# Layernorm of x + residual on one core: loads ahead of the opening barrier, no closing barriers, compute loops of 4 rows instead of 8

## The chip, the cores and the metric

The kernel runs on one core of one Trainium2 chip. The metric is the time of one execution in device microseconds (us). Each execution also has a *span*: the time from the first to the last instruction that the profiler recorded on that core. The timed figure is longer than the span of the same execution by 1.3 to 2.2 us; this document calls the difference *the time outside the span*, and it turns out to matter.

The engines are PE (matrix products), ACT, DVE and POOL (arithmetic on rows), and SP, which here only issues transfers; a *q* behind a name (SPq) marks instructions of the engine's own sequencer, PEld the loading of weights. A *DMA* is a transfer between memory and the chip's buffers. A *barrier* lets no engine go on before all have reached it; a *drain* is an instruction that stands in front of one. A *turn* is one pass of a loop, and a *junk buffer* takes an output that nobody reads, where only the accumulated sum is wanted.

## The reference, cut to what matters

```python
batch, seq, dim = 16, 1024, 512          # x, residual: float32; out: float32
z = x + residual
mean = np.mean(z, axis=-1, keepdims=True)
var  = np.var(z, axis=-1, keepdims=True)
return gamma * (z - mean) / np.sqrt(var + eps) + beta
```

There are 16,384 rows of 512 elements. With 128 partitions, each partition holds 128 rows; "a row" below means one such row on all partitions (256 KB). Two inputs are read and one output is written, 100.67 MB in all.

## The kernel before

The kernel is written by hand inside a critical section of a tile context: every engine has its own instruction stream, and semaphores tie them together. SP issues all large DMAs on one queue; POOL adds; ACT computes mean and sum of squares; DVE normalizes in place; SP stores. These are the parts that the change touches:

```python
TURN = 8                                  # rows per iteration of the ACT and DVE loops
JUNK = 4
...
ctx.enter_context(tc.tile_critical())
...
for c, (lo, n) in enumerate(loads_x):     # SP: loads of 8 rows (2 MB), stores of 16 rows (4 MB),
    ...                                   # at the end stores of 8, 4 and 4 rows
    nc.sync.dma_start(out=part(zbuf, Z_ROWS, lo, n), in_=dram(xf, lo, n)).then_inc(sx[c], 16)
    ...
with act.Fori(0, turns) as t:             # ACT, 8 rows a turn
    act.wait_ge(s_add, r0 + TURN)
    for k in range(2 * TURN):             # 8 means, then 8 sums of squares
        ...
        i.then_inc(s_act, 1).wait_op(s_act, due, "sem-ge")
    act.activation(out=std[...], in_=ssq[...], func=ACT.Sqrt, ...)...
with dve.Fori(0, turns) as t:             # DVE, 8 rows a turn
    for k in range(TURN):
        ...                               # each row waits for its own sum of squares
        dve.scalar_tensor_tensor(... nm ... gamma_p ...).wait_op(s_act, due, "sem-ge")
    dve.reciprocal(...)
    for k in range(TURN):
        dve.scalar_tensor_tensor(... rstd ... beta_p ...).then_inc(s_out, 1)
for o, (lo, n) in enumerate(stores):      # SP: wait for the last stores, clear all semaphores
    if lo >= stored:
        nc.sync.wait_ge(so[o], 16)
...
nc.sync.sem_clear(range(nums[0], nums[-1] + 1))
# leaving the critical section and the tile context adds the closing barriers
```

Of the kernel before, what the change touches and what calls it, by code (L numbers as in the profile page):

```python
# [6 lines left out]

FP32 = mybir.dt.float32
ACT = mybir.ActivationFunctionType
ALU = mybir.AluOpType  # L10


X_CHUNKS = [8] * 15 + [4, 4]
R_CHUNKS = [8] * 15 + [4, 4]
OUT_CHUNKS = [16] * 7 + [8, 4, 4]

Z_ROWS = 64
R_ROWS = 32
STORE_LAG = 40


TURN = 8


JUNK = 4


@with_exitstack
def kernel(
# [9 lines left out]
    nc = tc.nc  # L39
    P = nc.NUM_PARTITIONS  # L40
    xf = x.flatten_outer_dims()
    rf = residual.flatten_outer_dims()
    of = out.flatten_outer_dims()
    N, D = xf.shape
    inv_d = 1.0 / float(D)
    total = N // P
    turns = total // TURN

    def spans(sizes):
        assert sum(sizes) == total  # L50
        return [(sum(sizes[:c]), n) for c, n in enumerate(sizes)]

    blocks = spans(OUT_CHUNKS)

    def dram(t, lo, n):

        b0, bn = next(b for b in blocks if b[0] <= lo and lo + n <= b[0] + b[1])
        v = t[P * b0 : P * (b0 + bn), :].rearrange("(p j) d -> p j d", p=P)
        return v[:, lo - b0 : lo - b0 + n, :].rearrange("p a b -> p (a b)")

    ctx.enter_context(tc.tile_critical())  # L61

    zbuf = nc.alloc_sbuf_tensor("zbuf", [P, Z_ROWS * D], FP32)
    rbuf = nc.alloc_sbuf_tensor("rbuf", [P, R_ROWS * D], FP32)
    gb_row = nc.alloc_sbuf_tensor("gb_row", [1, 2 * D], FP32)
# [3 lines left out]
    nm = nc.alloc_sbuf_tensor("nm", [P, total], FP32)  # L69
    ssq = nc.alloc_sbuf_tensor("ssq", [P, total], FP32)  # L70
# [1 line left out]
    rstd = nc.alloc_sbuf_tensor("rstd", [P, total], FP32)  # L72
    gamma_p = nc.alloc_psum_tensor("gamma_p", [P, D], FP32)
    beta_p = nc.alloc_psum_tensor("beta_p", [P, D], FP32)
    junk = [nc.alloc_psum_tensor(f"junk{i}", [P, D], FP32) for i in range(JUNK)]

    sems = []

    def sem(name):
        s = nc.alloc_semaphore(name)  # L80
        sems.append(s)
        return s

    loads_x, loads_r, stores = spans(X_CHUNKS), spans(R_CHUNKS), spans(OUT_CHUNKS)
    sx = [sem(f"sx{c}") for c in range(len(loads_x))]
    sr = [sem(f"sr{c}") for c in range(len(loads_r))]
    so = [sem(f"so{c}") for c in range(len(stores))]
    s_gb = [sem(f"gb{k}") for k in range(2)]
    s_const = sem("const")
    s_pe = sem("pe")  # L90
    s_add = sem("add")
    s_act = sem("act")
    s_std = sem("std")
    s_dve = sem("dve")
    s_out = sem("out")

    def part(buf, size, lo, n):
        assert lo % size + n <= size
        return buf[:, (lo % size) * D : (lo % size + n) * D]


    nc.scalar.dma_start(out=gb_row[:, :D], in_=gamma[None, :]).then_inc(s_gb[0], 16)
    nc.scalar.dma_start(out=gb_row[:, D:], in_=beta[None, :]).then_inc(s_gb[1], 16)
    nc.vector.memset(ones[:, :], 1.0).then_inc(s_const, 1)  # L104
    nc.vector.memset(eps_t[:, :], float(eps)).then_inc(s_const, 1)  # L105
    nc.tensor.wait_ge(s_const, 1)
# [6 lines left out]

    todo_r, todo_o = list(enumerate(loads_r)), list(enumerate(stores))
    seen = {"add": 0, "out": 0}

    def wait_rows(s, key, rows):
        if rows > seen[key]:
            nc.sync.wait_ge(s, rows)
            seen[key] = rows  # L120

    stored = 0
    for c, (lo, n) in enumerate(loads_x):
        asked = lo + n
        while stored < asked - Z_ROWS:
            o = next(i for i, b in enumerate(stores) if b[0] == stored)
            assert all(o != t[0] for t in todo_o)
            nc.sync.wait_ge(so[o], 16)
            stored += stores[o][1]
        nc.sync.dma_start(  # L130
            out=part(zbuf, Z_ROWS, lo, n), in_=dram(xf, lo, n)
        ).then_inc(sx[c], 16)
        while todo_r and todo_r[0][1][0] + todo_r[0][1][1] <= asked:
            rc, (rlo, rn) = todo_r.pop(0)
            wait_rows(s_add, "add", rlo + rn - R_ROWS)
            nc.sync.dma_start(  # L136
                out=part(rbuf, R_ROWS, rlo, rn), in_=dram(rf, rlo, rn)
            ).then_inc(sr[rc], 16)
        while todo_o and (
            todo_o[0][1][0] + todo_o[0][1][1] <= asked - STORE_LAG or asked == total  # L140
        ):
            oc, (olo, on) = todo_o.pop(0)
            wait_rows(s_out, "out", olo + on)
            nc.sync.dma_start(  # L144
                out=dram(of, olo, on), in_=part(zbuf, Z_ROWS, olo, on)
            ).then_inc(so[oc], 16)


    have_x = have_r = 0
    lo = 0  # L150
    while lo < total:
        n = min(loads_x[have_x][1], loads_r[have_r][1])
        nc.gpsimd.wait_ge(sx[have_x], 16)
        nc.gpsimd.wait_ge(sr[have_r], 16)
        assert loads_x[have_x] == loads_r[have_r] == (lo, n)
        z = part(zbuf, Z_ROWS, lo, n)
        nc.gpsimd.tensor_tensor(  # L157
            out=z, in0=z, in1=part(rbuf, R_ROWS, lo, n), op=ALU.add
        ).then_inc(s_add, n)
        have_x, have_r, lo = have_x + 1, have_r + 1, lo + n  # L160

    def row_at(zoff, k):
        return zbuf[:, bass.ds(zoff + k * D, D)]


    act = nc.scalar
    act.preload_act_table_set("sqrt_and_others")  # L167
    act.wait_ge(s_const, 2)
    act.sem_inc(s_act, JUNK)
    with act.Fori(0, turns) as t:  # L170
        zoff = act.snap((t * (TURN * D)) % (Z_ROWS * D))
        r0 = act.snap(t * TURN)

        n0 = act.snap(t * (2 * TURN))
        act.wait_ge(s_add, r0 + TURN)
        for k in range(2 * TURN):
            row = k % TURN


            due = act.lower_val(n0 + (k + 1))  # L180
            if k < TURN:
                i = act.activation(  # L182
                    out=junk[k % JUNK][:, :],
                    in_=row_at(zoff, row),
                    func=ACT.Identity,
                    scale=-inv_d,
                    accum_out=nm[:, bass.ds(r0 + row, 1)],
                )
            else:
                i = act.activation(  # L190
                    out=junk[k % JUNK][:, :],
                    in_=row_at(zoff, row),
                    func=ACT.Square,
                    bias=nm[:, bass.ds(r0 + row, 1)],
                    accum_out=ssq[:, bass.ds(r0 + row, 1)],
                )
            i.then_inc(s_act, 1).wait_op(s_act, due, "sem-ge")
        due = act.lower_val(n0 + (JUNK + 2 * TURN))
        act.activation(  # L199
            out=std[:, bass.ds(r0, TURN)],  # L200
            in_=ssq[:, bass.ds(r0, TURN)],
            func=ACT.Sqrt,
            bias=eps_t[:, 0:1],
            scale=inv_d,
        ).then_inc(s_std, TURN).wait_op(s_act, due, "sem-ge")


    dve = nc.vector
    dve.wait_ge(s_pe, 2)
    with dve.Fori(0, turns) as t:  # L210
        zoff = dve.snap((t * (TURN * D)) % (Z_ROWS * D))
        r0 = dve.snap(t * TURN)
        n0 = dve.snap(t * (2 * TURN))
        for k in range(TURN):
            due = dve.lower_val(n0 + (JUNK + TURN + k + 1))
            dve.scalar_tensor_tensor(  # L216
                out=row_at(zoff, k),
                in0=row_at(zoff, k),
                scalar=nm[:, bass.ds(r0 + k, 1)],
                in1=gamma_p[:, :],  # L220
                op0=ALU.add,
                op1=ALU.mult,
            ).wait_op(s_act, due, "sem-ge")
        due = dve.lower_val(r0 + TURN)
        dve.reciprocal(  # L225
            out=rstd[:, bass.ds(r0, TURN)], in_=std[:, bass.ds(r0, TURN)]
        ).then_inc(s_dve, TURN).wait_op(s_std, due, "sem-ge")
        for k in range(TURN):
            i = dve.scalar_tensor_tensor(  # L229
                out=row_at(zoff, k),  # L230
                in0=row_at(zoff, k),
                scalar=rstd[:, bass.ds(r0 + k, 1)],
                in1=beta_p[:, :],
                op0=ALU.mult,
                op1=ALU.add,
            )
            i.then_inc(s_out, 1)
            if k == 0:
                i.wait_op(s_dve, due, "sem-ge")


    for o, (lo, n) in enumerate(stores):
        if lo >= stored:
            nc.sync.wait_ge(so[o], 16)
    nums = sorted(s.num for s in sems)
    assert nums == list(range(nums[0], nums[-1] + 1)), nums
    nc.sync.sem_clear(range(nums[0], nums[-1] + 1))


# [33 lines left out]
```

## Time and profile before

| | before |
|---|---|
| timed, median of 3 | 242.63 us (242.59 to 242.68) |
| profiled execution: timed / span | 242.21 / 240.03 us |
| DMA in the middle (24 to 180 us) | 430 GB/s |
| ACT, DVE, POOL busy | 74%, 74%, 59% |
| first load issued / its first packet | 0.94 / 1.96 us |
| last packet / last store's semaphore seen / end of span | 238.29 / 238.77 / 240.03 us |

The view by windows gives, for a stretch of time (us from the span's start), its length, the busy time of PE, PEld, DVE, ACT and POOL with the number of instructions, the clock, the mean busy share of the 16 DMA engines, and GB/s. Of the kernel before:

```profile
24.00:180.00 156.00, 0.00 (x0) 0.00 (x0) 137.24 (x209) 139.00 (x420) 105.70 (x13) 1.00 1.01 430
228.00:231.00 3.00, 0.00 (x0) 0.00 (x0) 3.00 (x5) 0.00 (x0) 0.00 (x0) 1.00 1.02 437
231.00:234.00 3.00, 0.00 (x0) 0.00 (x0) 0.11 (x1) 0.00 (x0) 0.00 (x0) 1.00 0.97 410
236.00:238.00 2.00, 0.00 (x0) 0.00 (x0) 0.00 (x0) 0.00 (x0) 0.00 (x0) 1.00 0.45 188
238.00:239.00 1.00, 0.00 (x0) 0.00 (x0) 0.00 (x0) 0.00 (x0) 0.00 (x0) 1.00 0.00 0
239.00:240.00 1.00, 0.00 (x0) 0.00 (x0) 0.00 (x0) 0.00 (x0) 0.00 (x0) 1.00 0.00 0
```

The DMA is saturated until about 236 us, even while the last rows are computed (228 to 231). The Trainium skill ("DMA: Bandwidth & Descriptors", Specifications) gives 435 GB/s as the ceiling of the fabric between the 16 DMA engines and the on-chip buffer; the 430 GB/s here agree. From 238 us on, nothing is moved and nothing is computed, yet the span goes on for two microseconds.

What fills these microseconds is in the sequencers' instructions. For one line of the source, this view gives engine, operation, count, shortest/median/longest duration in ns, and the start of the first and of the last one in us. Line 278 is the tile context, line 247 the clearing of semaphores:

```profile
L247 SPq EVENT_SEMAPHORE_RANGE_CLEAR  x1: 115/115/115, 238.8 to 238.8; - x1
...
L278 POOLq EVENT_SEMAPHORE  x4: 17/17/17, 239.4 to 239.9; - x4
...
L278 SPq DRAIN  x3: 7/7/7, 239.3 to 239.6; - x3
...
L278 SPq EVENT_SEMAPHORE  x2: 17/17/17, 239.5 to 240.0; - x2
```

After the last store's semaphore at 238.77, SP clears (238.83), and then two rounds of drains and barriers of the tile context follow, preceded by a handshake of the critical section. Each instruction takes 7 to 115 ns; from 238.77 to the end of the span it is 1.26 us.

The start, in the timeline (start us, duration us, engine, line, operation; lines of other engines cut):

```profile
0.94 0.39 SPq L130 DMA_DIRECT2D zbuf<-in_x_dram  x1
...
1.38 0.43 SPq L136 DMA_DIRECT2D rbuf<-in_residual_dram  x1
...
1.86 0.42 SPq L130 DMA_DIRECT2D zbuf<-in_x_dram  x1
```

Finally the compute loop. In the chain that ended last (start us, duration us, what), ACT's seven merged steps of sums of squares come once a turn:

```profile
30.77 2.32 ACT junk L190 x7
...
42.20 2.32 ACT junk L190 x7
...
53.59 2.31 ACT junk L190 x7
```

So a turn of 8 rows takes ACT 42.20 - 30.77 = 11.43 us. The DMA needs 6.29 MB / 430 GB/s = 14.6 us for the same rows, so compute has slack.

### The profile page before, as it was taken

The numbers are of one execution on the slowest core, as the hardware profiler recorded it, in microseconds if no ns is written. First come the engines' busy times: TensorE is split into PE (matmuls) and PEld (weight loads), VectorE is DVE, ScalarE is ACT, GpSimd is POOL, SyncE is SP. The second block draws the span as 40 slices with busy tenths as digits, with TensorE's granted clock in tenths as the row PEclk, the third lists the DMA queues.
The fourth block names the chain that finished last, engine by engine and source line by source line (L and its number), as shares of the span: only waits on it lengthen the run. The fifth ranks groups of instructions, "written<-read, shape, count | busy, mean of one in ns | idle before, by whom it ended". The sixth has DMA issues, their size and how long they took to land.

```text
span 240.0 us, 1853 instructions
## 1 busy us (share of the span) xinstructions
PE 4.1 (2%) x4; PEld 1.0 (0%) x4; DVE 178.7 (74%) x274; ACT 176.6 (74%) x529; POOL 142.2 (59%) x21
## 2 busy tenths in 40 slices
PE   3300000000000000000000000000000000000000
PEld 0000000000000000000000000000000000000000
DVE  0000399999999999999997399944999359995950
ACT  2002999999999999999972999449993599959500
POOL 0078989889899506894088920989109890860000
DMA  7999999999999999999999999999999999999994
GB/s 252 434 420 429 431 435 431 429 415 431 434 440 437 415 420 431 475 437 390 429 434 434 420 426 434 429 453 426 415 423 431 456 399 423 445 426 431 431 418 205
DMA packets 6341, 100.68 MB, mean 419 GB/s; under 512 B 706, under 2 KB 706, under 8 KB 708
## 3 DMA queue, kind: packets, MB, share of 16 engines
q1 hardware_dynamic: 6336, 100.67, 98.4%
q14 instruction: 1, 0.01, 0.0%
q10 hardware_dynamic: 4, 0.00, 0.0%
HBM read 67.11 MB, written 33.55 MB: 419 GB/s over the span
## 4 chain that ended last, share of the span: by engine, by line
DMA 56%; ACT 14%; issue 14%; POOL 6%; DVE 3%; SPq 2%; ACTq 2%; DVEq 0%; POOLq 0%
DMA out_dram<-zbuf 36%; DMA rbuf<-in_residual_dram 20%; ACT junk L190 9%; POOL zbuf L157 6%; ACT junk L182 5%; DVE zbuf L229 3%; SPq L130 1%; ACTq L180 1%; ACTq L182 1%; SPq L136 1%; ACT std L199 0%; SPq L144 0%; DVE rstd L225 0%; DVEq L229 0%; ACTq L170 0%
## 5 line engine op out<-in xcount | busy, mean ns | idle before, releaser
L157 POOL TENSOR_TENSOR zbuf<-zbuf,rbuf 128x4096 f32<-128x4096 f32 (+1 forms) x17 | 142.0, 8351 | 71.5 <-DMA rbuf<-in_residual_dram 71.5
L216 DVE SCALAR_TENSOR_TENSOR zbuf<-zbuf,nm,gamma_p 128x512 f32 x128 | 91.0, 747 | 50.8 <-ACT junk L190 50.8
L182 ACT ACTIVATE junk<-zbuf 128x512 f32 x128 | 74.4, 581 | 45.3 <-POOL zbuf L157 41.6
L229 DVE SCALAR_TENSOR_TENSOR zbuf<-zbuf,rstd,beta_p 128x512 f32 x128 | 85.7, 743 | 0.6
L190 ACT ACTIVATE junk<-zbuf,nm 128x512 f32 x128 | 86.1, 673 | 0.0
L190 ACT ACTIVATION_READ_ACCUMULATOR junk<-zbuf,nm x128 | 24.2, 189 | 0.0
L182 ACT ACTIVATION_READ_ACCUMULATOR junk<-zbuf x128 | 23.9, 187 | 0.0
L199 ACT ACTIVATE std<-ssq,eps_t x16 | 4.8, 301 | 1.6
L225 DVE RECIPROCAL rstd<-std x16 | 3.1, 196 | 0.0
L167 ACT ACT_TABLE_LOAD x1 | 1.3, 1283 | 1.7 <-SPq L61 1.7
L109 PE MATMUL beta_p<-gb_row,ones 1*128 1x512 f32 x2 | 2.1, 1136 | 2.4 <-DMA gb_row<-in_beta_dram 2.4
L109 PE MATMUL gamma_p<-gb_row,ones 1*128 1x512 f32 x2 | 2.0, 1122 | 2.3 <-DMA gb_row<-in_gamma_dram 2.3
L104 DVE MEMSET ones<- 1x128 f32 x1 | 0.2, 165 | 1.0 <-SPq L61 1.0
L109 PEld LDWEIGHTS beta_p<-gb_row,ones 1*128 1x128 f32 x2 | 0.5, 304 | 4.0 <-DMA gb_row<-in_beta_dram 4.0
L109 PEld LDWEIGHTS gamma_p<-gb_row,ones 1*128 1x128 f32 x2 | 0.5, 305 | 2.3 <-issue 2.3
L264 POOL MEMSET const-float32-0.0<- 128x1 f32 x1 | 0.1, 99 | 0.2 <-issue 0.2
L264 POOL MEMSET const-bfloat16-1.0<- 128x1 bf16 x1 | 0.1, 102 | 0.0
L264 POOL MEMSET const-uint8-127<- 128x1 uint8 x1 | 0.1, 102 | 0.0
L264 POOL MEMSET const-float32-1.0<- 128x1 f32 x1 | 0.1, 99 | 0.0
L105 DVE MEMSET eps_t<- 128x1 f32 x1 | 0.1, 59 | 0.0
## 6 DMA issues: line engine op xcount, KB each, us to landing
zbuf<-in_x_dram SPq DMA_DIRECT2D x15, 2048.0 KB, 32.8
rbuf<-in_residual_dram SPq DMA_DIRECT2D x15, 2048.0 KB, 30.4
out_dram<-zbuf SPq DMA_DIRECT2D x7, 4096.0 KB, 28.5
zbuf<-in_x_dram SPq DMA_DIRECT2D x2, 1024.0 KB, 32.6
rbuf<-in_residual_dram SPq DMA_DIRECT2D x2, 1024.0 KB, 34.6
out_dram<-zbuf SPq DMA_DIRECT2D x1, 2048.0 KB, 16.5
out_dram<-zbuf SPq DMA_DIRECT2D x2, 1024.0 KB, 7.7
gb_row<-in_gamma_dram ACTq DMA_DIRECT2D x1, 2.0 KB
```

The costliest lines, as they stand in the source:

```text
L109: nc.tensor.matmul(dest[:, :], ones[:, :], gb_row[:, k * D : (k + 1) * D], start=True, stop=True).then_inc(s_pe, 1)
L130: nc.sync.dma_start(out=part(zbuf, Z_ROWS, lo, n), in_=dram(xf, lo, n)).then_inc(sx[c], 16)
L136: nc.sync.dma_start(out=part(rbuf, R_ROWS, rlo, rn), in_=dram(rf, rlo, rn)).then_inc(sr[rc], 16)
L157: nc.gpsimd.tensor_tensor(out=z, in0=z, in1=part(rbuf, R_ROWS, lo, n), op=ALU.add).then_inc(s_add, n)
L167: act.preload_act_table_set("sqrt_and_others")
L180: due = act.lower_val(n0 + (k + 1))
L182: i = act.activation(out=junk[k % JUNK][:, :], in_=row_at(zoff, row), func=ACT.Identity, scale=-inv_d, accum_out=nm[:, bass.ds(r0 + row, 1)],)
L190: i = act.activation(out=junk[k % JUNK][:, :], in_=row_at(zoff, row), func=ACT.Square, bias=nm[:, bass.ds(r0 + row, 1)], accum_out=ssq[:, ...
L199: act.activation(out=std[:, bass.ds(r0, TURN)], in_=ssq[:, bass.ds(r0, TURN)], func=ACT.Sqrt, bias=eps_t[:, 0:1], scale=inv_d,).then_inc(s ...
L216: dve.scalar_tensor_tensor(out=row_at(zoff, k), in0=row_at(zoff, k), scalar=nm[:, bass.ds(r0 + k, 1)], in1=gamma_p[:, :], op0=ALU.add, op1 ...
L225: dve.reciprocal(out=rstd[:, bass.ds(r0, TURN)], in_=std[:, bass.ds(r0, TURN)]).then_inc(s_dve, TURN).wait_op(s_std, due, "sem-ge")
L229: i = dve.scalar_tensor_tensor(out=row_at(zoff, k), in0=row_at(zoff, k), scalar=rstd[:, bass.ds(r0 + k, 1)], in1=beta_p[:, :], op0=ALU.mul ...
```

## The change

Its intent: the first two loads shall be in flight before the opening barrier; nothing shall follow the last store but one small clear; the loops shall run 4 rows a turn with fewer register instructions. The tile context is closed and compiled empty at the kernel's start, so its barriers come first, and everything else is placed by hand behind it.

```diff
-TURN = 8
-JUNK = 4
+ADD = 8
+TURN = 4
+EARLY = 2
...
+    tc.close()
+    tc.compile()
...
-    ctx.enter_context(tc.tile_critical())
...
-    junk = [nc.alloc_psum_tensor(f"junk{i}", [P, D], FP32) for i in range(JUNK)]
+    junk_m = [...]        # one per row of a turn; two of the eight in SBUF
+    junk_s = [...]
...
+    def move(out, in_, s):
+        i = nc.sync.dma_start(out=out, in_=in_).then_inc(s, 16)
+        if len(first) < EARLY:
+            first.append(i.ins)
...
+    for o, (lo, n) in enumerate(stores[:-1]):
+        if lo >= stored:
+            nc.sync.wait_ge(so[o], 16)
+    nc.sync.sem_clear(range(nums[0], nums[-1]))
+    nc.sync.wait_ge(so[-1], 16)
+    nc.sync.sem_clear(range(nums[-1], nums[-1] + 1))
...
     # ACT: instead of a wait on every instruction
+        act.wait_ge(s_act, r0 * 2 + TURN)          # all means, then the squares
+        act.wait_ge(s_act, r0 * 2 + 2 * TURN)      # all squares, then the square root
...
     # DVE: instead of a wait on every row
+        dve.wait_ge(s_act, r0 * 2 + 2 * TURN)
...
+    blks = nc.main_func.blocks                     # the first two loads go ahead of the
+    names = {i.name for i in first}                # opening block's first Drain
+    ...
+    blks[0].instructions = opening[:at] + first + opening[at:]
```

More of the change, by code (lines that the diff above doesn't have):

```diff
@@ L6 @@
 from concourse._compat import with_exitstack
+from concourse.ordered_engine_set import OrderedEngineSet
 FP32 = mybir.dt.float32
@@ L74 @@
     beta_p = nc.alloc_psum_tensor("beta_p", [P, D], FP32)
-    junk = [nc.alloc_psum_tensor(f"junk{i}", [P, D], FP32) for i in range(JUNK)]
+    junk_m = [nc.alloc_psum_tensor(f"junk_m{i}", [P, D], FP32) for i in range(TURN)]
+    junk_s = [nc.alloc_psum_tensor(f"junk_s{i}", [P, D], FP32) for i in range(6 - TURN)]
+    junk_s += [
+        nc.alloc_sbuf_tensor(f"junk_s{i}", [P, D], FP32) for i in range(6 - TURN, TURN)
+    ]
     sems = []
@@ L82, in sem @@
         return s
-    loads_x, loads_r, stores = spans(X_CHUNKS), spans(R_CHUNKS), spans(OUT_CHUNKS)
+    loads_x, loads_r, stores = spans(X_CHUNKS), spans(R_CHUNKS), blocks
     sx = [sem(f"sx{c}") for c in range(len(loads_x))]
     sr = [sem(f"sr{c}") for c in range(len(loads_r))]
-    so = [sem(f"so{c}") for c in range(len(stores))]
     s_gb = [sem(f"gb{k}") for k in range(2)]
@@ L95 @@
     s_out = sem("out")
+    so = [sem(f"so{c}") for c in range(len(stores))]
+    nums = [s.num for s in sems]
+    assert nums == list(range(nums[0], nums[-1] + 1)), nums
     def part(buf, size, lo, n):
@@ L99, in part @@
         return buf[:, (lo % size) * D : (lo % size + n) * D]
-    nc.scalar.dma_start(out=gb_row[:, :D], in_=gamma[None, :]).then_inc(s_gb[0], 16)
-    nc.scalar.dma_start(out=gb_row[:, D:], in_=beta[None, :]).then_inc(s_gb[1], 16)
+    for k, src in enumerate((gamma, beta)):
+        nc.scalar.dma_start(out=gb_row[:, k * D : (k + 1) * D], in_=src[None, :]).then_inc(
+            s_gb[k], 16
+        )
     nc.vector.memset(ones[:, :], 1.0).then_inc(s_const, 1)
@@ L115 @@
     seen = {"add": 0, "out": 0}
+    first = []
     def wait_rows(s, key, rows):
@@ L129 @@
             stored += stores[o][1]
-        nc.sync.dma_start(
-            out=part(zbuf, Z_ROWS, lo, n), in_=dram(xf, lo, n)
-        ).then_inc(sx[c], 16)
+        move(part(zbuf, Z_ROWS, lo, n), dram(xf, lo, n), sx[c])
         while todo_r and todo_r[0][1][0] + todo_r[0][1][1] <= asked:
@@ L135 @@
             wait_rows(s_add, "add", rlo + rn - R_ROWS)
-            nc.sync.dma_start(
-                out=part(rbuf, R_ROWS, rlo, rn), in_=dram(rf, rlo, rn)
-            ).then_inc(sr[rc], 16)
+            move(part(rbuf, R_ROWS, rlo, rn), dram(rf, rlo, rn), sr[rc])
         while todo_o and (
@@ L143 @@
             wait_rows(s_out, "out", olo + on)
-            nc.sync.dma_start(
-                out=dram(of, olo, on), in_=part(zbuf, Z_ROWS, olo, on)
-            ).then_inc(so[oc], 16)
-    have_x = have_r = 0
-    lo = 0
-    while lo < total:
-        n = min(loads_x[have_x][1], loads_r[have_r][1])
-        nc.gpsimd.wait_ge(sx[have_x], 16)
-        nc.gpsimd.wait_ge(sr[have_r], 16)
-        assert loads_x[have_x] == loads_r[have_r] == (lo, n)
-        z = part(zbuf, Z_ROWS, lo, n)
-        nc.gpsimd.tensor_tensor(
-            out=z, in0=z, in1=part(rbuf, R_ROWS, lo, n), op=ALU.add
-        ).then_inc(s_add, n)
-        have_x, have_r, lo = have_x + 1, have_r + 1, lo + n
-    def row_at(zoff, k):
-        return zbuf[:, bass.ds(zoff + k * D, D)]
+            move(dram(of, olo, on), part(zbuf, Z_ROWS, olo, on), so[oc])
+    for o, (lo, n) in enumerate(stores[:-1]):
[4 more added lines that the diff above has]
+    nc.sync.sem_clear(range(nums[-1], nums[-1] + 1))
+    for c, (lo, n) in enumerate(loads_x):
+        nc.gpsimd.wait_ge(sx[c], 16)
+        for rc, (rlo, rn) in enumerate(loads_r):
+            if lo <= rlo < lo + n:
+                assert rlo + rn <= lo + n
+                nc.gpsimd.wait_ge(sr[rc], 16)
+                for a in range(rlo, rlo + rn, ADD):
+                    an = min(ADD, rlo + rn - a)
+                    z = part(zbuf, Z_ROWS, a, an)
+                    nc.gpsimd.tensor_tensor(
+                        out=z, in0=z, in1=part(rbuf, R_ROWS, a, an), op=ALU.add
+                    ).then_inc(s_add, an)
     act = nc.scalar
@@ L168 @@
     act.wait_ge(s_const, 2)
-    act.sem_inc(s_act, JUNK)
     with act.Fori(0, turns) as t:
@@ L172 @@
         r0 = act.snap(t * TURN)
-        n0 = act.snap(t * (2 * TURN))
         act.wait_ge(s_add, r0 + TURN)
-        for k in range(2 * TURN):
-            row = k % TURN
-            due = act.lower_val(n0 + (k + 1))
-            if k < TURN:
-                i = act.activation(
-                    out=junk[k % JUNK][:, :],
-                    in_=row_at(zoff, row),
-                    func=ACT.Identity,
-                    scale=-inv_d,
-                    accum_out=nm[:, bass.ds(r0 + row, 1)],
-                )
-            else:
-                i = act.activation(
-                    out=junk[k % JUNK][:, :],
-                    in_=row_at(zoff, row),
-                    func=ACT.Square,
-                    bias=nm[:, bass.ds(r0 + row, 1)],
-                    accum_out=ssq[:, bass.ds(r0 + row, 1)],
-                )
-            i.then_inc(s_act, 1).wait_op(s_act, due, "sem-ge")
-        due = act.lower_val(n0 + (JUNK + 2 * TURN))
+        for k in range(TURN):
+            act.activation(
+                out=junk_m[k][:, :],
+                in_=zbuf[:, bass.ds(zoff + k * D, D)],
+                func=ACT.Identity,
+                scale=-inv_d,
+                accum_out=nm[:, bass.ds(r0 + k, 1)],
+            ).then_inc(s_act, 1)
+        act.wait_ge(s_act, r0 * 2 + TURN)
+        for k in range(TURN):
+            act.activation(
+                out=junk_s[k][:, :],
+                in_=zbuf[:, bass.ds(zoff + k * D, D)],
+                func=ACT.Square,
+                bias=nm[:, bass.ds(r0 + k, 1)],
+                accum_out=ssq[:, bass.ds(r0 + k, 1)],
+            ).then_inc(s_act, 1)
+        act.wait_ge(s_act, r0 * 2 + 2 * TURN)
         act.activation(
@@ L204 @@
             scale=inv_d,
-        ).then_inc(s_std, TURN).wait_op(s_act, due, "sem-ge")
+        ).then_inc(s_std, TURN)
     dve = nc.vector
@@ L212 @@
         r0 = dve.snap(t * TURN)
-        n0 = dve.snap(t * (2 * TURN))
+        dve.wait_ge(s_act, r0 * 2 + 2 * TURN)
         for k in range(TURN):
-            due = dve.lower_val(n0 + (JUNK + TURN + k + 1))
+            row = zbuf[:, bass.ds(zoff + k * D, D)]
             dve.scalar_tensor_tensor(
-                out=row_at(zoff, k),
-                in0=row_at(zoff, k),
+                out=row,
+                in0=row,
                 scalar=nm[:, bass.ds(r0 + k, 1)],
@@ L222 @@
                 op1=ALU.mult,
-            ).wait_op(s_act, due, "sem-ge")
-        due = dve.lower_val(r0 + TURN)
+            )
+        dve.wait_ge(s_std, r0 + TURN)
         dve.reciprocal(
             out=rstd[:, bass.ds(r0, TURN)], in_=std[:, bass.ds(r0, TURN)]
-        ).then_inc(s_dve, TURN).wait_op(s_std, due, "sem-ge")
+        ).then_inc(s_dve, TURN)
+        dve.wait_ge(s_dve, r0 + TURN)
         for k in range(TURN):
-            i = dve.scalar_tensor_tensor(
-                out=row_at(zoff, k),
-                in0=row_at(zoff, k),
+            row = zbuf[:, bass.ds(zoff + k * D, D)]
+            dve.scalar_tensor_tensor(
+                out=row,
+                in0=row,
                 scalar=rstd[:, bass.ds(r0 + k, 1)],
@@ L235 @@
                 op1=ALU.add,
-            )
-            i.then_inc(s_out, 1)
-            if k == 0:
-                i.wait_op(s_dve, due, "sem-ge")
-    for o, (lo, n) in enumerate(stores):
-        if lo >= stored:
-            nc.sync.wait_ge(so[o], 16)
-    nums = sorted(s.num for s in sems)
-    assert nums == list(range(nums[0], nums[-1] + 1)), nums
-    nc.sync.sem_clear(range(nums[0], nums[-1] + 1))
+            ).then_inc(s_out, 1)
+    blks = nc.main_func.blocks
+    names = {i.name for i in first}
+    for b in blks[1:]:
+        kept = [i for i in b.instructions if i.name not in names]
+        if len(kept) < len(b.instructions):
+            b.instructions = kept
+    opening = list(blks[0].instructions)
+    at = next(n for n, i in enumerate(opening) if i.opcode == "Drain")
+    blks[0].instructions = opening[:at] + first + opening[at:]
 _INS = ['x', 'residual', 'gamma', 'beta', 'eps']
```

## The prediction

> **What bounds it now.** The DMA. The windows view gives 430 GB/s at a DMA share of about 1.00 from 24 to 180 us, and 423 to 441 in every window from 4 to 231. The Trainium skill ("DMA: Bandwidth & Descriptors", Specifications) gives 435 GB/s as the fabric ceiling of the 16 engines; this trace sits at it: 100.67 MB at 430 GB/s are 234 us of a 240.0 us span. ACT and DVE are busy 74% each, POOL 59%. One turn of 8 rows takes ACT 11.4 us where it runs without a gap (chain of waits, 23 to 80 us), but 8 rows are 6.29 MB, 14.6 us of DMA. Bytes issued against bytes landed: the queue never holds less than about 3.7 MB in the middle and 1.4 MB (3.3 us) at the end, so it never runs dry.
>
> What is not DMA is at the ends (timeline with the sequencers' instructions). The opening barrier and the jump take 0.0 to 0.82 us, the first load is issued at 0.94, its first packet is at 1.96. The last packet ends at 238.29, the last store's semaphore is seen at 238.77, and clearing semaphores (0.12 us) and closing barriers run until 240.0. The timed runs are 2.6 us longer than the span (242.63 against 240.0), which I carry over.
>
> **What the change does.**
> - First two loads ahead of the opening barrier: first issue from 0.94 to about 0.0, first packet from 1.96 to about 1.0. Two issues (0.39 + 0.43 us) delay the barrier for the rest, and the third load comes at perhaps 1.5 to 2.5 us; the 4.2 MB ahead of it last 9.8 us, so that is hidden. Critical: about -0.9 us.
> - No closing barriers: 238.77 to 240.03 is 1.26 us; one small clear remains, about 0.2. Critical: about -1.0 us. Engines done early might also shorten what follows the span; I count 0.2.
> - Turns of 4 rows: the ACT turn's fixed part is 11.39 - 8 x (0.61 + 0.71) = 0.85 us. Twice as many turns and a whole wait between means and squares give an estimated 12.7 us per 8 rows; DVE, which now starts after all squares, an estimated 12.5. Both stay under 14.6, so nothing reaches the DMA. At the end rows come out in finer pieces and the last stores are issued earlier, but the queue is not empty there in either kernel: worth 0.
> - Junk buffers in SBUF, semaphore order: off the path.
>
> **Prediction.** 242.63 - 0.9 - 1.0 - 0.2 is 240.5 us (0.991 of before). 8 in 10: 239.2 to 241.7. Faster by over 2% (below 237.8): 0.03; within 2%: 0.95; slower by over 2%: 0.02.
>
> **What would show it right.** First DMA issue at 0.0, first packet near 1.0 us; DMA still 428 to 432 GB/s in the middle; last packet near 237.4; the span ending 0.6 to 0.8 us after the last packet instead of 1.74, near 238.0. An ACT turn of 6.2 to 6.6 us. The large waits of the DMA queue stay waits for landed stores.
>
> **What would make it wrong.** The drain in the opening barrier might wait for the loads issued before it (about 10 us later): third load and compute start late, the queue runs dry, some us slower. The last engine's straggling packets (16 streams until 236.7, one until 238.3) may fall otherwise, +-0.7 us. A turn of 4 might cost ACT or DVE over 14.6 us per 8 rows. Or the time outside the span may change with the barriers.

## The result, and the profile after

Ratios here are the mean time of one kernel's runs over the mean of the other's runs of the same rounds, so they are not quite the ratio of the medians quoted.

| | before | after |
|---|---|---|
| timed, median of 4 | 242.61 us | 239.62 us (239.49 to 239.69) |
| ratio | | 0.9879, 95% interval 0.9862 to 0.9896 |
| profiled: timed / span | 242.21 / 240.03 | 239.69 / 238.37 |
| timed less span, same execution | 2.18 | 1.32 |
| first issue / first packet | 0.94 / 1.96 | 0.00 / 1.00 |
| last packet / end of span | 238.29 / 240.03 | 237.87 / 238.37 |

The windows of the kernel after:

```profile
24.00:180.00 156.00, 0.00 (x0) 0.00 (x0) 135.66 (x222) 144.72 (x426) 105.40 (x13) 1.00 1.01 430
...
228.00:231.00 3.00, 0.00 (x0) 0.00 (x0) 2.75 (x5) 0.00 (x0) 0.00 (x0) 1.00 0.97 415
231.00:234.00 3.00, 0.00 (x0) 0.00 (x0) 0.00 (x0) 0.00 (x0) 0.00 (x0) 1.00 0.99 418
234.00:236.00 2.00, 0.00 (x0) 0.00 (x0) 0.00 (x0) 0.00 (x0) 0.00 (x0) 1.00 0.98 414
236.00:238.00 2.00, 0.00 (x0) 0.00 (x0) 0.00 (x0) 0.00 (x0) 0.00 (x0) 1.00 0.06 25
238.00:238.40 0.40, 0.00 (x0) 0.00 (x0) 0.00 (x0) 0.00 (x0) 0.00 (x0) 1.00 0.00 0
```

The middle is unchanged at 430 GB/s. The share of 0.06 in the window 236 to 238 is about what a single DMA engine gives (one sixteenth is 0.0625); it works on alone after the others have finished.

The sequencers' instructions: line 169 is the last clear, line 55 the closing of the empty tile context, whose barriers now stand at the start:

```profile
L169 SPq EVENT_SEMAPHORE_RANGE_CLEAR  x1: 25/25/25, 238.3 to 238.3; - x1
...
L55 POOLq EVENT_SEMAPHORE  x4: 17/17/17, 1.4 to 1.8; - x4
...
L55 SPq DRAIN  x3: 7/7/7, 1.3 to 1.6; - x3
```

The start in the timeline:

```profile
0.00 0.38 SPq L138 DMA_DIRECT2D zbuf<-in_x_dram  x1
0.43 0.42 SPq L138 DMA_DIRECT2D rbuf<-in_residual_dram  x1
1.91 0.33 SPq L138 DMA_DIRECT2D zbuf<-in_x_dram  x1
```

ACT's merged steps of sums of squares in the chain that ended last; some groups between them are left out:

```profile
24.80 2.31 ACT junk_s L203 x7
...
31.02 2.31 ACT junk_s L203 x7
...
37.23 2.31 ACT junk_s L203 x7
```

The first two loads are issued at 0.00 and 0.43; the third waits until 1.91 for three barriers, but at its issue 4.2 MB are still outstanding, so the queue is not empty. SP's drain behind the two issues (0.91 us) took 125 ns, against 7 ns in before; it did not wait for the loads, which landed from 7.5 us on. A turn of 4 rows takes ACT 6.2 us (31.02 - 24.80), or 12.4 per 8 rows: more than the 11.4 of before, still below 14.6.

The profiles add up as follows. First packet: -0.96 us. From the last packet to the end of the span: 1.74 to 0.51, -1.24 us. From the first packet to the last: 236.33 to 236.87, +0.54 us. Together -1.66 us of span. Outside the span: -0.86 us. The sum is -2.52 us for these two executions. The profile of before was taken in one of its fastest executions (242.21, against medians of 242.38 to 242.88 in the later rounds), which makes the +0.54 look larger than it is on the average. It lies in the lag of one straggling DMA engine (last experiment): 1.52 us in this execution of after and 0.83 in this one of before.

### The profile page after: what moved, and what is told of

It reads as the page before. It is cut to its first block, busy times and chain, and to the rows that moved or that the text cites. A ratio compares the mean times of both kernels' runs of the same rounds, so it can differ in the third digit from the quotient of the medians.

```text
span 238.4 us, 1803 instructions
## 1 busy us (share of the span) xinstructions
PE 3.7 (2%) x4; PEld 1.2 (0%) x4; DVE 177.2 (74%) x290; ACT 186.5 (78%) x545; POOL 142.2 (60%) x21
## 4 chain that ended last, share of the span: by engine, by line
ACT 38%; DMA 33%; issue 10%; POOL 7%; ACTq 5%; DVE 3%; SPq 1%; DVEq 0%; POOLq 0%
DMA rbuf<-in_residual_dram 21%; ACT junk_s L203 20%; ACT junk_m L194 18%; DMA out_dram<-zbuf 12%; POOL zbuf L181 7%; ACTq L194 2%; DVE zbuf L228 2%; DVE zbuf L243 1%; ACTq L203 1%; SPq L138 1%; ACTq L189 1%; ACT std L211 0%; ACTq L201 0%; ACTq L210 0%; DVEq L228 0%
## 5 line engine op out<-in xcount | busy, mean ns | idle before, releaser
L228 DVE SCALAR_TENSOR_TENSOR zbuf<-zbuf,nm,gamma_p 128x512 f32 x128 | 87.1, 743 | 50.4 <-ACT junk_s L203 50.4
L194 ACT ACTIVATE junk_m<-zbuf 128x512 f32 x128 | 74.9, 585 | 28.5 <-POOL zbuf L181 23.3
L203 ACT ACTIVATE junk_s<-zbuf,nm 128x512 f32 x128 | 88.8, 694 | 3.9
L243 DVE SCALAR_TENSOR_TENSOR zbuf<-zbuf,rstd,beta_p 128x512 f32 x128 | 87.1, 744 | 1.1
L203 ACT ACTIVATION_READ_ACCUMULATOR junk_s<-zbuf,nm x128 | 23.9, 187 | 0.0
L194 ACT ACTIVATION_READ_ACCUMULATOR junk_m<-zbuf x128 | 23.9, 187 | 0.0
L211 ACT ACTIVATE std<-ssq,eps_t x32 | 9.5, 297 | 3.7
L237 DVE RECIPROCAL rstd<-std x32 | 5.4, 170 | 0.0
```

The lines of the kernel that those rows point to most:

```text
L194: act.activation(out=junk_m[k][:, :], in_=zbuf[:, bass.ds(zoff + k * D, D)], func=ACT.Identity, scale=-inv_d, accum_out=nm[:, bass.ds(r0 + ...
L203: act.activation(out=junk_s[k][:, :], in_=zbuf[:, bass.ds(zoff + k * D, D)], func=ACT.Square, bias=nm[:, bass.ds(r0 + k, 1)], accum_out=ss ...
L211: act.activation(out=std[:, bass.ds(r0, TURN)], in_=ssq[:, bass.ds(r0, TURN)], func=ACT.Sqrt, bias=eps_t[:, 0:1], scale=inv_d,).then_inc(s ...
L228: dve.scalar_tensor_tensor(out=row, in0=row, scalar=nm[:, bass.ds(r0 + k, 1)], in1=gamma_p[:, :], op0=ALU.add, op1=ALU.mult,)
L237: dve.reciprocal(out=rstd[:, bass.ds(r0, TURN)], in_=std[:, bass.ds(r0, TURN)]).then_inc(s_dve, TURN)
L243: dve.scalar_tensor_tensor(out=row, in0=row, scalar=rstd[:, bass.ds(r0 + k, 1)], in1=beta_p[:, :], op0=ALU.mult, op1=ALU.add,).then_inc(s_ ...
```

## The experiments

Twelve runs were made (eleven new kernels, and the kernel after once more), in three batches of five rounds on three chips. "Before" was timed in every batch: means 242.67, 242.82 and 242.38 us, spans 240.50, 240.65 and 240.20, outside the span 2.17, 2.16 and 2.18. The table gives each kernel's mean difference from before in its own rounds, split into span and outside; the last column is the mean time outside.

| run | timed, us | span | outside | time outside, us |
|---|---|---|---|---|
| after, run again | -2.71 | -1.85 | -0.86 | 1.32 |
| before, loads early | -0.72 | -0.74 | +0.02 | 2.19 |
| before, turns of 4 | -0.26 | +0.16 | -0.42 | 1.76 |
| same, ACT padded | -0.02 | +0.39 | -0.40 | 1.76 |
| same, DVE padded | +0.12 | +0.33 | -0.21 | 1.95 |
| before, ACT 4 rows, DVE 8 | +0.34 | +0.36 | -0.02 | 2.16 |
| after, no early loads | -1.24 | -0.37 | -0.87 | 1.30 |
| after, one barrier at the end | -1.93 | -1.56 | -0.37 | 1.80 |
| after, ACT and DVE padded | -2.70 | -1.98 | -0.72 | 1.46 |
| after, last waits on PE | -2.00 | -1.40 | -0.60 | 1.58 |
| after, turns of 8 | -1.96 | -1.12 | -0.84 | 1.32 |
| after, last store in two | -2.10 | -1.23 | -0.86 | 1.30 |

The time outside the span repeats within about 0.1 us from execution to execution (except in the DVE-padded kernel, below), so it can be compared much more finely than the total. Spans are on record to 0.1 us, and they scatter: a difference of mean spans carries a standard error of 0.06 to 0.24 us, so one of 0.2 or 0.3 us proves little by itself.

**The loads alone.** The kernel before, with its first two loads moved ahead of the opening block's first drain after the tile context is compiled:

```diff
+    blks = nc.main_func.blocks
+    first = [...the first two DMAs of SP...]
+    ...
+    blks[0].instructions = opening[:at] + first + opening[at:]
```

> The kernel before with only its first two loads moved ahead of the opening barrier; closing barriers kept. My theory: first packet near 1.0 instead of 1.96, so -0.9 us: 241.5 to 241.9, and the timed run stays about 2.2 to 2.6 us longer than the span. Rival for the time outside the span (it shrank because of the start): it is then 1.3 us here, and the time is 240.6 to 241.0.

Measured: 241.85 us (ratio 0.9971, interval 0.9957 to 0.9984); first packet at 1.02 us; outside 2.19. The early loads are worth 0.7 us where the first packet moved by 0.94, and nothing outside the span. The missing 0.2 is not clear of the scatter (standard error 0.15). The rival is out.

**The change without early loads.**

```diff
-EARLY = 2
+EARLY = 0
```

> The kernel after with no load ahead of the opening barrier (the two barriers of the empty tile context then stand before the first load). My theory: first issue at about 1.4 us, first packet at about 2.4, 239.6 + 1.4 = 241.0 us (240.7 to 241.3), and the timed run still only 1.3 us longer than the span. Rival for the time outside the span (the start): 2.2 or more outside, 241.9 us or more.

Measured: 241.29 us (0.9942); first issue at 1.39 us, because the empty context's two barriers now stand in front of it; outside 1.30. Against after, by their differences from before, the span is longer by 1.85 - 0.37 = 1.48 us, for a first packet that is 1.40 later (2.40 against 1.00). The standard error is about 0.25: one of the six executions was 1.2 us above the others, and without it the difference is 1.27. So a later first packet costs about as much as it is late, and the empty context's barriers are free only because two loads go ahead of them.

**A barrier put back at the end.**

```diff
+    nc.all_engine_barrier()
```

> The kernel after with one barrier of all engines put back at its end, so that the four engines that are done early must wait for the last store. My theory (the time outside the span shrank because those engines do their own end of program while the last store is still on its way): span +0.3 to +0.5, and outside the span from 1.3 back to 2.2 or more, 240.7 to 241.3 us. Rival (it comes from elsewhere): outside stays 1.3, 239.9 to 240.1 us.

Measured: 240.60 us (0.9918); span 0.29 us above after (by the differences), outside 1.80 instead of 1.30. One barrier thus costs 0.3 us inside the span (in the traces, 0.77 us from the last packet to the end of the span instead of 0.51) and another 0.5 us outside it. The traces of before and after show the difference that the barrier restores: in after the last instruction of PE begins at 9.2 us, of POOL at 208.8, of ACT at 225.2 and of DVE at 230.0, and SP alone goes on to 238.4; in before all five go on to 239.9 or later. The theory holds in kind: engines that are held until the last store has landed add something after the span. But the time did not return to 2.2, so another 0.4 us of the 0.87 has another cause.

**Turns of 4 alone.**

```diff
-TURN = 8
+TURN = 4
```

> The kernel before with compute loops of 4 rows and nothing else. My theory (DMA-bound, queue never empty; the turn is worth 0): 242.3 to 242.9 us, ratio 0.998 to 1.002, span about 240.0, the last two stores issued some us earlier, the last packet within 0.7 us of 238.3. Rival (finer turns shorten the tail and carry part of the 3.0 us): 241.6 us or less.

Measured: 242.43 us (0.9990, interval 0.9977 to 1.0004). The total is in the expected range, but for a reason that the theory did not have: the span is slightly *longer* (+0.16) and the time outside is shorter by 0.42 us. So the missing 0.4 goes with the size of the loops. In its trace the last two stores are issued at 222.9 and 229.0 us instead of 228.5 and 231.1, earlier as expected, but the last packet ends at 239.42, outside the expected 0.7 around 238.3: the straggler lags by 1.89 us there, against 0.83 in the trace of before.

**Which program's length?** With turns of 4, ACT's program falls from 63 to 43 instructions and DVE's from 60 to 40. Two kernels put the length back, with turns of 4, on one engine each, ahead of its loop:

```diff
     act.sem_inc(s_act, JUNK)
+    for _ in range(24):
+        act.sem_inc(s_pad, 1)
```
```diff
     dve.wait_ge(s_pe, 2)
+    for _ in range(24):
+        dve.sem_inc(s_pad, 1)
```

> The kernel before with turns of 4 and, on ACT alone, 24 extra semaphore instructions ahead of its loop (67 ACT instructions in the program; before has 63, with turns of 4 it has 43). The time outside the span was 2.17 us in before and 1.76 with turns of 4. Theory: a long ACT program needs one more instruction fetch (8 KB), which the end of the program waits for: outside back to 2.1 to 2.2 us, and a fetch of 8 KB shows again in the trace. Rival (it is DVE's program, or not a matter of program length): outside stays 1.7 to 1.8.

> The same with the 24 instructions on DVE alone (64 DVE instructions; before has 60, with turns of 4 it has 40). Theory of ACT: outside stays 1.7 to 1.8 us. Rival of DVE: 2.1 to 2.2.

Measured: ACT padded, 1.76 outside, no change, although an 8 KB instruction fetch did appear again, at 31.97 us. DVE padded: six executions with 2.06, 1.82, 2.19, 1.74, 2.15 and 1.76 outside, half of them as in before and half as with turns of 4. The theory of ACT is out; DVE is implicated, but a padded program is not quite the same thing as a longer loop. The profile of one of the long executions has an 8 KB instruction fetch 1.8 us after the end of its span. But the profiles of before and of the loads alone, with 2.18 and 2.13 us outside, have none there, so the fetch is not shown to be the cause.

> The kernel before with the loop of 4 rows on ACT alone; DVE keeps its loop of 8 (60 DVE instructions in the program, as before; 43 on ACT). Theory after the padded runs: it is DVE's program that makes the 0.4 us outside the span, so 2.1 to 2.2 us outside, as in before. Rival (both programs count, or the loop of ACT): 1.7 to 1.8 outside. Span 240.2 to 241.0.

In this kernel ACT runs 4 rows a turn and DVE 8, and DVE's waits are re-counted for that:

```diff
+ATURN = 4                       # stands for TURN everywhere in ACT's loop
...
-            due = dve.lower_val(n0 + (JUNK + TURN + k + 1))
+            due = dve.lower_val(n0 + (JUNK + (k // ATURN + 1) * ATURN + k + 1))
```

Measured: 242.68 us (1.0015, interval 1.0001 to 1.0028), outside 2.16. That settles the engine for kernels that keep the closing barriers: with DVE's loop of 8 rows the time outside is that of before, whatever ACT does. This profile too has no instruction fetch after its span.

**The same length in the kernel after.**

```diff
     act.wait_ge(s_const, 2)
+    for _ in range(28):
+        act.sem_inc(s_pad, 1)
...
     dve.wait_ge(s_pe, 2)
+    for _ in range(28):
+        dve.sem_inc(s_pad, 1)
```

> The kernel after with 28 extra semaphore instructions on ACT and on DVE ahead of their loops (63 and 60 instructions in the program, as before). Theory: both engines are done some us before the last store, so a longer end of program there is hidden: 1.3 us outside the span, 239.4 to 240.0 us, as the kernel after beside it. Rival (a long program costs 0.4 us whoever is last): 1.7 outside, 239.8 to 240.4.

Measured: 239.70 us, the same as after beside it (239.66); outside 1.46 instead of 1.32. What a longer DVE program adds outside is mostly hidden when DVE is done before the last store has landed (its last instruction begins at 230.3 us, the store lands at 238.3), as the theory says, though 0.14 us of it shows.

The kernel after itself, unchanged, ran beside it:

> The kernel after itself again, in the same rounds as the next three. All theories: 239.4 to 240.0 us, span 238.1 to 238.8, 1.3 us outside the span. One stream of the 16 lags by 1 to 3 us at the end, and its lag is what the runs differ by.

Measured: 239.66 us (0.9888, interval 0.9873 to 0.9904), 1.32 outside. The result repeats in another batch, on chip 7.

**Another engine last.**

```diff
-    nc.sync.wait_ge(so[o], 16) ...            # SP waits for the last stores and clears
+    last = nc.tensor
+    last.wait_ge(s_out, total)
+    for o, (lo, n) in enumerate(stores):
+        if lo >= stored:
+            last.wait_ge(so[o], 16)
+    last.sem_clear(range(nums[0], nums[-1] + 1))
```

> The kernel after with the last waits and the clearing of semaphores on PE instead of SP, so that SP too is done early. If the time outside the span is the end of program of whichever engine ends last, it changes with the engine: PE against SP, 1.0 to 1.6 us, and the total with it. If it is common to all engines and starts when the last one is done, it stays 1.3 us: 239.4 to 240.1 us.

Measured: 240.36 us; outside 1.58 instead of 1.32, and the span is 0.45 us longer, in which PE's clear takes 447 ns, where SP's first clear took 118 and its last 25. (The edit also puts the whole clear behind the last store; SP had done all but one semaphore before.) What follows the span depends on which engine ends last, and SP is the better one of the two.

**Turns of 8 in the new form.** The junk buffers are eight, shared by means and squares.

```diff
-TURN = 4
+TURN = 8
...
+    junk_m = [nc.alloc_psum_tensor(f"junk{i}", [P, D], FP32) for i in range(6)]
+    junk_m += [nc.alloc_sbuf_tensor(f"junk{i}", [P, D], FP32) for i in range(6, TURN)]
+    junk_s = junk_m
```

> The kernel after with turns of 8 (six junk buffers in PSUM and two in SBUF, shared by means and squares). My theory: span as in after, 238.0 to 238.6 us, since the queue never runs dry; outside the span 1.3 us, since ACT and DVE are done long before the last store and whatever they fetch is hidden: 239.3 to 239.9 us. Rival 1 (turns of 4 shorten the end by more than that): over 240.1. Rival 2 (long programs cost 0.4 us outside whoever is last): outside 1.7, 239.9 to 240.2.

Measured: 240.73 us (0.9920); outside 1.32, as the theory had it, but the span is 0.73 us longer than that of after. Rival 1 is right, and the windows of this kernel show how:

```profile
228.00:231.00 3.00, 0.00 (x0) 0.00 (x0) 2.96 (x7) 0.00 (x0) 0.00 (x0) 1.00 1.02 437
231.00:234.00 3.00, 0.00 (x0) 0.00 (x0) 3.00 (x5) 0.00 (x0) 0.00 (x0) 1.00 0.16 66
234.00:236.00 2.00, 0.00 (x0) 0.00 (x0) 1.50 (x3) 0.00 (x0) 0.00 (x0) 1.00 1.04 430
```

From 231 to 234 the DMA is at 0.16: the queue has run dry and waits for DVE. At 66 instead of 430 GB/s about 2.5 us of transfer are lost in this window. The span grows by less (1.06 us between these two profiles), since the straggler has caught up in the pause: at the last store its lag is 0.02 us here and 1.52 in after. Setting issued bytes against landed bytes, nothing is outstanding at 233.2, when the second last store is issued; in after there are 3.1 MB outstanding at the same store's issue (224.9) and 1.2 at the last one's (231.1). The reason is the wait of the new form: DVE may start a turn only when all its squares are done. In before, where each row waits for its own square, DVE's first pass overlaps ACT's squares, and turns of 8 were no loss. The last turn of DVE, first in before and then in this kernel:

```profile
219.93 5.68 DVE L216 SCALAR_TENSOR_TENSOR zbuf<-zbuf,nm,gamma_p 128x512 f32 x8 [2.63 <-ACT junk L190]
...
225.76 5.36 DVE L229 SCALAR_TENSOR_TENSOR zbuf<-zbuf,rstd,beta_p 128x512 f32 x8
```
```profile
224.64 5.36 DVE L226 SCALAR_TENSOR_TENSOR zbuf<-zbuf,nm,gamma_p 128x512 f32 x8 [2.73 <-ACT junk L201]
...
230.14 5.36 DVE L241 SCALAR_TENSOR_TENSOR zbuf<-zbuf,rstd,beta_p 128x512 f32 x8
```

Here it starts 4.7 us later, after ACT's last square, which itself ended no later (224.4 and 224.8 us). No run changed this wait alone. So turns of 4 are worth nothing in the old form of the loop and are needed in the new one.

**The straggling engine.** In before and after one stream of the 16 ends later than all others. For each DMA, the time between its fifteenth and its sixteenth completion grows from 0.06 and 0.07 us for the first load to 0.83 us (before) and 1.52 us (after) for the last store. The difference between the two need not be the kernels': over all the traces whose queue stayed full and whose last store was whole, the lag runs from 0.83 to 1.98 us (1.56 in after run again, 1.98 with the loads alone). From the first packet to the last, less this lag, all of them take 235.3 to 235.7 us. If the engine is the last of the 16, it can be spared by a store over 120 partitions: the Trainium skill ("DMA: Bandwidth & Descriptors", Why a DMA increments its semaphore by 16 and not by 1) says that the largest divisor up to 16 sets the number of engines and that the lowest-numbered ones are used, so that is the first 15.

```diff
-            move(dram(of, olo, on), part(zbuf, Z_ROWS, olo, on), so[oc])
+            if olo + on == total:
+                move(d_[:120], s_[:120], so[oc])
+                move(d_[120:], s_[120:], so[oc])
...
-    nc.sync.wait_ge(so[-1], 16)
+    nc.sync.wait_ge(so[-1], 32)
```

> The kernel after with its last store (4 rows) as two, of 120 and of 8 partitions. In after one of the 16 streams ends 1.5 us behind the second last, and its lag grows by about 0.3 us with each large store. If the 120 partitions go to the first 15 engines (the Trainium skill, DMA: Bandwidth & Descriptors, Why a DMA increments its semaphore by 16) and the lagging engine is the last, it has 64 KB, about 2.4 us, less to do, and the span falls to 236.9 to 237.5 us. If the lagging engine is another one, the others of the first eight get 8 KB more, and the span rises by about 0.3 us to 238.4 to 238.9.

Measured: 240.78 us (0.9910), a miss; the span is 0.62 us longer than that of after by the differences from before. The trace agrees with the page on the number of engines: the last store's semaphore gets two increments right after the issues and 23 later on, as 15 and 8 engines would give. It also narrows down the straggler. At the end one stream alone moves 8 KB packets of 0.31 us each, signals the end of its share of the first part (seen at 239.50 us, where all other streams are done with both parts by 238.11), then moves one packet more and signals its share of the second part (239.81). So the straggler is one of the eight engines that have a share in both parts, and the split gave it 0.31 us more to do. If these eight are the lowest-numbered ones, as the page says and no run here shows, it is not the sixteenth. The rest of the 0.62 us is in the lag, which was 2.35 us at the store before (1.44 in after). Which of the eight it is stays open.

None of these kernels beats the kernel after; the padded one equals it.

## Why the prediction was right

The time, 239.62 us, lies in the range of 239.2 to 241.7 and the class (within 2%) is right. It lies near the lower end of that range. The middle of 240.5 was 0.9 too high, and one term accounts for 0.66 of that; the span itself fell by 1.85 us in the mean, where the prediction's 0.9 and 1.0 make 1.9.

- **The DMA is the bound, and a saved microsecond at either end counts.** Right. 430 GB/s in the middle of both kernels; without early loads, the first packet comes 1.40 us later and the span is 1.48 longer (standard error about 0.25). SP's largest wait stays the one for landed stores (110.9 us in before, 109.8 in after), as predicted.
- **First two loads: -0.9.** Right in the trace (first packet -0.96). Done alone, they gave -0.72 us.
- **No closing barriers: -1.0.** Right in kind, a little small: from the last packet to the end of the span it is -1.24 us; I had allowed 0.6 to 0.8 us there, and it took 0.51.
- **Outside the span: "I count 0.2".** This is the term that was mis-sized. It is 0.86 us. What the runs show in its place: engines that are done before the last store lands no longer add to the time after the span. One barrier put back, with DVE's short loop, restores 0.5 of it; DVE's loop of 8 rows adds the other 0.4 where all engines wait for the end (b_dve8 against turns of 4). Where DVE does not wait, its loop hardly counts: turns of 8 in the new form have 1.32 outside. So the barriers' removal seems to carry nearly all of the 0.86, and the shorter loops little or none; the kernel before without its closing barriers and with nothing else changed was not run. I had also read the size wrongly: I subtracted the span of one execution from the median of others (242.63 - 240.0 = 2.6), where the same execution gave 242.21 - 240.03 = 2.18.
- **Turns of 4 worth 0.** Right in the total for the old form of the loop, but by luck, as two small things that I did not foresee nearly cancel: +0.2 to +0.4 us of span (four kernels with turns of 4 on ACT have +0.16 to +0.39, the first of them within the scatter) and -0.4 outside. ACT's turn of 6.2 us is at the lower edge of the predicted 6.2 to 6.6. I missed that the coarser waits of the new form make the shorter turn necessary: with turns of 8 the queue runs dry between 231 and 234 us and 0.73 us are lost.
- **The last engine's straggling as a risk of ±0.7.** Right as a size: the stream from first to last packet is 0.54 us longer in the profile of after, and the straggler's lag (1.52 against 0.83) makes up 0.69. The span of before alone varies from 240.0 to 241.1 us.

What stays open: why DVE's long loop costs 0.4 us after the span (an instruction fetch was seen there in one execution, but not in the profiles of before, the loads alone and b_dve8, whose time outside is as long); why turns of 4 on ACT lengthen the span by 0.2 to 0.4 us (in the traces of the four the straggler lags by 1.33 to 1.96 us, against 0.83 in before, but by 1.98 with the loads alone, which have turns of 8); and which of eight DMA engines straggles, and why its lag grows.

## What to carry to other kernels

When the DMA is saturated from the first packet to the last, only what comes before the first packet and after the last one can be saved: issue the first loads before any barrier, let one engine alone wait for the last store, and let the other engines end early: the time outside the span was 1.3 us with that and 2.2 without. Even then one DMA engine that lags behind the other 15 can set the end. Compare timed runs and spans of the *same* executions, because a change can act outside what the profile shows. Where waits are made coarser, as in this loop, shorter turns may be needed; check that the last stores are still issued while bytes are outstanding.

## What the Trainium skill lacked or had wrong

- "Runtime: NRT & Kernel Launch" (The ~15µs preamble/postamble breakdown) lists stages at the end of a kernel but not how they lie when the engines end at different times: the time outside the span was 1.30 us with only SP waiting, 1.58 with PE waiting, 1.80 with a barrier at the end, and 2.17 with the closing barriers of before and a DVE loop of 8 rows.
- The same page (Instruction fetch mechanics) calls crossing a block of instructions mostly hidden. In before, an 8 KB fetch at 33.15 us took 0.31 us of one DMA engine, and the last completion of the following loads then lagged by 0.31 us instead of 0.06, up to about 100 us; by 145 us it was 0.03. No run shows that this reaches the end of the kernel: after, without such a fetch, and its padded form, with one at 28.5 us, took 239.66 and 239.70 us.
- "DMA: Bandwidth & Descriptors" says nothing of one engine falling behind over a run without DMAs issued by GpSimd: the lag grew to 0.83 us in before and to 1.52 in after. Its first-byte latency of about 0.6 us (Specifications) agrees if counted from the end of the issue (0.38 to 1.00 us in after); from the start of the issue it is 1.0.
- No page that I read gives the cost of clearing a range of semaphores by engine: 447 ns on PE, 115 to 121 on SP for a range of some fifty.
- "VectorE: DVE Perf Modes" (The DRAIN you can't avoid) gives about 12 ns for the drains that the runtime adds at a program's start and end, and nothing for those of a program's own barriers. SP's drain directly behind two DMA issues took 125 ns in after (7 without early loads); the others of before and after took 7 to 64, POOL's behind its memsets 186 to 188.
